# Two-layer hybrid decoder trunk: Silu on ScalarE, two-bank adds into x, and 18 more pairs of the feed-forward blocks computed by seven products

## The chip, the cores and the metric

The kernel runs on one core of one Trainium2 chip. The metric is device time in microseconds (us) of one execution. The kernel before takes 2581.33 us (median of 3 runs, 2581.15 to 2582.71).

A core has engines with instruction queues of their own: TensorE (PE in the profile; PEld is its loading of weights), VectorE (DVE), ScalarE (ACT), GpSimd (POOL) and SyncE (SP, which here issues most of the DMAs). Instructions on one engine run in the order of its queue; engines wait for each other by semaphores. Matmuls write to PSUM, eight banks of 512 fp32 columns by 128 partitions; everything else lies in SBUF.

## The reference, cut to what matters

For `x` of 256 tokens by 2048 columns, in fp32:

- Layer 0: `x += mixer(norm(x))`. The mixer is one input projection (`l0_w_in`, 2048 x 12336), eight mLSTM heads, 32 Mamba-2 (SSD) heads with a short convolution and a gate `y * silu(z)`, and one output projection (`l0_w_out`).
- Layer 1: `x += attention(norm(x))`. With 256 tokens and blocks of 256 this is causal attention over one block, 16 heads of 128 with rotary positions (`l1_w_qkv`, `l1_w_o`).
- After either mixer a feed-forward block: `x += (silu(n @ w_gate) * (n @ w_up)) @ w_down` with `n = norm(x)`, where `w_gate` and `w_up` are 2048 x 5632 and `w_down` is 5632 x 2048.
- A last norm, then the output. Every norm is `x * rsqrt(mean(x*x) + 1e-6) * gain`.

`silu(a)` is `a * sigmoid(a)`, which is also `a/2 * (1 + tanh(a/2))`.

## The kernel before, in words

**Precision.** Every fp32 operand of a large matmul is split in two: a high part, which ScalarE writes by rounding (a copy to the type fp32r), and a low part, which VectorE writes as the operand less the high part. A product is then three matmuls (high by high, high by low, low by high). For a weight tile the high part is `wh` (L439), the low part `wl` (L441); the three matmuls are L472, L473 and L474.

**Tiling.** Activations stand transposed as K tiles (128 of the inner dimension by 256 tokens, high and low), four to a block of a `KT` object. `block` (L456) makes a 256-token by 1024-column result: two strips of 512 columns (of gate and of up in the first half of a feed-forward block, two neighbours elsewhere) by two tiles of 128 tokens, so four PSUM banks F[0] to F[3]. It runs over pairs of K tiles. A pair of kind P costs 4 results x 2 K tiles x 3 matmuls = 24 matmuls of 512 columns. A pair of kind S computes the same 2 x 2 block product with Strassen's (Winograd's form) seven products instead of eight: 7 x 3 = 21 matmuls. For that VectorE makes four sums of the weights (L448, L449, L451: `sums`, which takes a second `raw` buffer), which are split as well, so an S pair has seven weight parts and a P pair four. Four sums of the activations (`skx`, `skh`, by `activation_sums`, L308) are made once for each pair of K tiles. Four of the seven products go into extra banks E (4 to 7); after a block's last S pair they are combined into four tiles `pre` (L510 to L514), which are added to F (L1007) or, with F, into x (L901).

**Plans.** A string tells the kind of each pair of a block. Blocks with 16 K tiles have eight pairs: `PLAN_X` ("PSPSPSPP", three S) for most, `PLAN_LATE` ("PPPSPSPP", two S) for the first block after a norm. `PLAN_H` is for `w_down`: "PSPSPPPP" (two S) for the groups of four hidden strips, "PSPSPP" for the last group of three. While a block is between its first and its last S pair (`held`), the short jobs put off by `later`, such as the transposes of finished hidden strips, are not run, since they use banks 6 and 7.

**A feed-forward block** (`ffn`, L992) goes over 11 hidden strips of 512 columns in groups of 4, 4 and 3. For each strip `hidden` runs one block for gate and up, adds `pre` and F, and makes h with one ScalarE instruction (Tanh, L1010) and two VectorE ones (L1011, L1012). The transposes of h are put off to just after the first pair of the next block. After a group two blocks (`add_blocks`, L893, the two halves of the 2048 columns) multiply by `w_down` and add into x.

**Buffers and order.** Weight tiles come from SyncE's DMAs into `raw` (three buffers and a fourth used every fourth time), `wh` and `wl` (three each). An S pair takes two of each, a P pair one. No order is written out by hand: a scheduler that simulates the program on its own cost model fixes each engine's order beforehand. It follows program order, and `tc.high_priority(offset=n)` lets what is inside go that much earlier (800 for the splits of weights, 1600 for the adds of F). PE's order is rearranged as well: in the trace, parts of a block's first S pair stand behind the next P pair.

**PSUM banks.** The accumulators of the projections that do not use `block` (`lin_w`, `lin_a`) take their banks one by one from a ring of six (`acc_bank`); `block` takes banks 0 to 3 for F. A bank is free for its next user when what is in it has been read.

Of the kernel before, what the change touches and what calls it, by code (L numbers as in the profile page):

```python
# [9 lines left out]
F32 = mybir.dt.float32  # L10
# [30 lines left out]
PLAN_H = {4: "PSPSPPPP", 3: "PSPSPP"}  # L41
# [4 lines left out]
FFN = ({"rawx": 1}, {"skh": 2}, {"blk": 4}, {"gf": 4})  # L46
# [19 lines left out]
def hybrid_trunk(ctx: ExitStack, tc: tile.TileContext, a: dict, out: bass.AP):  # L66
# [88 lines left out]
    ring = {"acc": (0, 1, 2, 3, 4, 5), "aux": (6, 7)}  # L155
# [40 lines left out]
    idle = acc_bank("p_idle")  # L196
# [111 lines left out]
    def activation_sums(a, gains):  # L308
# [6 lines left out]
        nc.vector.tensor_sub(sf[:, 3, :], a12, sf[:, 1, :])  # L315
        if gains:
            sk = small([P, 4, 2, P], "skx", F32R)
        else:
            sk = held_tile("skh", [P, 4, 2, P], "skh", F32R)
        split(sk[:, :, 0, :], sk[:, :, 1, :], sf)  # L320
        return sk

    def sums_of(kt, j):
# [4 lines left out]
        nc.vector.tensor_add(xg, pair[:, :, 0, :].bitcast(F32), pair[:, :, 1, :].bitcast(F32))
        kt.sums[j] = activation_sums(xg, True)
# [40 lines left out]
    def lin_w(w, col, kt, nk, ready=None):  # L370
# [4 lines left out]
        banks = [acc_bank("acc_w") for _ in range(4)]  # L375
# [80 lines left out]
    def block(src, kt, row, nk, plan, after_sums=None, lead=1, pairs=None, ahead=()):  # L456
# [22 lines left out]
        for i_, j in enumerate(order):  # L479
# [58 lines left out]
        return F, pre  # L538
# [354 lines left out]
    def add_blocks(w, kt, row, nk, plans, finish=None, begin=None, whole=None, pairs=None, ahead=((), ())):  # L893

        for q in range(2):
# [3 lines left out]
            def add_all(what):  # L899
                for d, x in zip(dst, what):  # L900
                    nc.vector.tensor_add(d, d, x)  # L901
# [5 lines left out]
            F, _ = block(((w, c0), (w, c0 + STRIP)), kt, row, nk, plans[q], add_all, 2 if final else 1, pairs and list(pairs),  # L907
# [10 lines left out]
            with tc.high_priority(offset=1600):  # L918
                add_all(F)
# [41 lines left out]
    for q in range(2):  # L961
        F, pre = block(tuple((w_in, C_Z + (2 * q + n) * STRIP) for n in range(2)), xt0, 0, KD, PLAN_X if q else PLAN_LATE,
# [29 lines left out]
    def ffn(xt, r, wg_, wu_, wd, name, finish, begin=None, whole=None):  # L992

        rh = cst.tile([P, NT], F32, tag="rh", name="rh" + name)
        rr = cst.tile([P, NT], F32, tag="rr", name="rr" + name)
        nc.vector.tensor_scalar(rh, r, 0.5, None, op0=OP.mult)
        nc.vector.tensor_mul(rr, rh, r)

        def hidden(hT, i, s, plan):
            F, pre = block(((wg_, s * STRIP), (wu_, s * STRIP)), xt, 0, KD, plan)  # L1000
            hs = []
            for t in range(NT):
                g, u = F[2 * t], F[2 * t + 1]
                if pre is not None:
                    for p, f in zip(pre[2 * t:2 * t + 2], (g, u)):
                        with tc.high_priority(offset=1600):
                            nc.vector.tensor_add(p, p, f)  # L1007
                    g, u = pre[2 * t:2 * t + 2]
                h = t2([P, STRIP], "h")
                nc.scalar.activation(h, g, AF.Tanh, scale=rh[:, t:t + 1])  # L1010
                nc.vector.scalar_tensor_tensor(h, h, 1.0, g, op0=OP.add, op1=OP.mult)  # L1011
                nc.vector.scalar_tensor_tensor(h, u, rr[:, t:t + 1], h, op0=OP.mult, op1=OP.mult)  # L1012
                hs.append(h)
# [94 lines left out]
    for q in range(2):  # L1108
        F, pre = block(tuple((w_qkv, 2 * D + (2 * q + n) * STRIP) for n in range(2)), xt2, 0, KD, PLAN_X if q else PLAN_LATE)
# [9 lines left out]
    turn["acc"] = 4  # L1119
# [15 lines left out]
    def begin_ffn1(s):  # L1135
        gain[s] = held_tile("gf", [P, STRIP], "gf")
# [60 lines left out]
```

## Time and profile before

| | |
|---|---|
| median of 3 runs | 2581.33 us |
| profiled execution, span from first to last instruction | 2578.2 us (its time by the measure of the runs isn't given apart; the median lies 3.1 us above its span) |
| PE busy | 2563.5 us, 99% of the span, 12222 matmuls |
| VectorE busy | 2196.5 us, 85% |
| ScalarE busy | 1454.3 us, 56% |
| mean granted TensorE clock | 0.999 |
| DMA | 496.55 MB, mean 193 GB/s |
| first feed-forward block | about 754 to 1460 us of the span |
| second feed-forward block | about 1871 to 2578 us of the span |

How to read it: "busy" is the time in which an engine has at least one instruction under way. Matmuls overlap in the pipeline (one is shown as 0.39 us long while the next starts 0.23 us after it), so a busy PE is no proof that it runs at its best rate; start-to-start times tell that. VectorE's instructions overlap by a little as well. Rows of groups give count, busy time, mean ns of one, then the engine's idle time just before them and what ended it.

### The profile page before, as it was taken

The page shows a single profiled execution, that of the slowest core. Times are in us where ns is not written, and L with a number is a line of the kernel's source. Part 1 is how long each engine was busy: PE and PEld are TensorE (multiplying, and loading weights), DVE is VectorE, ACT ScalarE, POOL GpSimd, SP SyncE. Part 2 cuts the span into 40 slices and gives each one's busy share as a digit, 9 for nine tenths or more (in the row PEclk, how much of TensorE's full clock was granted, in tenths as well). Part 3 has the DMA queues.
Part 4 walks back from the last instruction along what each step waited for, and adds up shares of the span by engine and source line. Part 5 has one row for each costly group of instructions (what it writes and reads, how often), then busy time and mean ns, then how long its engine had stood idle before and what let it go on. Part 6 is the DMA issues. An engine that isn't in the chain of part 4 may idle for free.

```text
span 2578.2 us, 32660 instructions
## 1 busy us (share of the span) xinstructions
PE 2563.5 (99%) x12222; PEld 2130.7 (83%) x12222; DVE 2196.5 (85%) x2831; ACT 1454.3 (56%) x1929; POOL 43.6 (2%) x77
## 2 busy tenths in 40 slices
PE   9999999999999999999999999999999999999998
PEld 8888888888888888888888888888888888888887
DVE  6676777799989998899889986767999888988898
ACT  6465665566665554555455665666655545554554
POOL 2000010000000000000000000000000000000000
PEclk9999999999999999999999999999999999999999
DMA  7566576566564656465656556554555655565554
GB/s 237 170 211 182 166 235 182 163 205 212 185 213 163 215 194 212 163 226 188 206 167 225 186 174 229 164 180 146 180 192 200 212 181 199 193 213 191 199 188 154
DMA packets 254767, 496.55 MB, mean 193 GB/s; under 512 B 15704, under 2 KB 16608, under 8 KB 254352
## 3 DMA queue, kind: packets, MB, share of 16 engines
q1 hardware_dynamic: 250384, 483.26, 57.1%
q0 software_dynamic: 2896, 8.51, 1.1%
q10 hardware_dynamic: 1328, 2.70, 0.3%
q8 instruction: 96, 1.57, 0.2%
q14 instruction: 63, 0.52, 0.1%
HBM read 492.26 MB, written 2.14 MB: 192 GB/s over the span
## 4 chain that ended last, share of the span: by engine, by line
PE 90%; DVE 5%; issue 2%; DMA 2%; ACT 1%; SPq 0%; POOL 0%; POOLq 0%; DVEq 0%; ACTq 0%
PE acc_f L473 18%; PE acc_f L474 18%; PE acc_f L472 17%; PE acc_w L381 11%; PE acc_w L385 5%; PE acc_e L472 4%; PE acc_e L473 4%; PE acc_e L474 4%; PE acc_a L412 2%; PE acc_a L413 2%; PE acc_a L411 2%; DVE wl L441 2%; PE p_tr L282 2%; PE p_y L866 1%; DMA raw<-in_l_w_o 1%
## 5 line engine op out<-in xcount | busy, mean ns | idle before, releaser
L439 ACT CAST wh<-raw 128x1024 fp32r<-128x1024 f32 (+1 forms) x577 | 630.0, 1134 | 412.9 <-PE acc_f L474 338.1
L441 DVE TENSOR_TENSOR wl<-raw,wh 128x1024 fp32r<-128x1024 f32 (+1 forms) x577 | 748.7, 1323 | 79.1 <-ACT wh L439 73.8
L474 PE MATMUL acc_f<-wh,x 128*128 128x512 f32 x1122 | 438.2, 391 | 0.0
L473 PE MATMUL acc_f<-wl,x 128*128 128x512 f32 x1122 | 437.5, 390 | 0.1
L472 PE MATMUL acc_f<-wh,x 128*128 128x512 f32 x1122 | 436.5, 391 | 0.0
L366 DVE TENSOR_TENSOR wl<-raw,wh 128x1024 fp32r<-128x1024 f32 (+1 forms) x225 | 271.3, 1218 | 139.8 <-ACT wh L365 137.3
L439 ACT CAST wh<-sums 128x1024 fp32r<-128x1024 f32 x222 | 227.9, 1051 | 225.9 <-PE acc_f L474 137.7
L365 ACT CAST wh<-raw 128x1024 fp32r<-128x1024 f32 (+1 forms) x225 | 231.9, 1044 | 196.3 <-PE acc_w L381 111.6
L441 DVE TENSOR_TENSOR wl<-sums,wh 128x1024 fp32r<-128x1024 f32 x222 | 266.7, 1221 | 34.6 <-ACT wh L439 34.1
L473 PEld LDWEIGHTS acc_f<-wl,x 128*128 128x128 f32 x1122 | 210.7, 188 | 44.9 <-DVE wl L441 1.9
L474 PEld LDWEIGHTS acc_f<-wh,x 128*128 128x128 f32 x1122 | 210.7, 188 | 43.1
L472 PEld LDWEIGHTS acc_f<-wh,x 128*128 128x128 f32 x1122 | 210.6, 188 | 42.6
L381 PE MATMUL acc_w<-xa,wh 128*128 128x512 f32 x768 | 207.5, 398 | 1.5 <-DVE xa L229 1.5
L381 PEld LDWEIGHTS acc_w<-xa,wh 128*128 128x128 f32 x768 | 138.8, 189 | 27.9 <-DVE xa L229 1.6
L448 DVE TENSOR_TENSOR sums<-raw 128x1024 f32<-128x1024 f32 x111 | 135.4, 1220 | 12.9 <-DMA raw<-in_l_ffn_up 8.0
L381 PE MATMUL acc_w<-x,wh 128*128 128x512 f32 x512 | 138.9, 399 | 0.0
L385 PE MATMUL acc_w<-xa,wl 128*128 128x256 f32 x768 | 121.8, 282 | 0.0
L385 PEld LDWEIGHTS acc_w<-xa,wl 128*128 128x128 f32 x768 | 110.1, 190 | 6.7
L474 PE MATMUL acc_f<-wh,hb 128*128 128x512 f32 (+1 forms) x284 | 109.6, 387 | 0.0
L473 PE MATMUL acc_f<-wl,hb 128*128 128x512 f32 (+1 forms) x284 | 109.6, 387 | 0.0
L472 PE MATMUL acc_f<-wh,hb 128*128 128x512 f32 (+1 forms) x284 | 109.5, 387 | 0.0
L472 PE MATMUL acc_f<-wh,ha 128*128 128x512 f32 x280 | 109.0, 390 | 0.0
(362 smaller groups left out, 4581.3 us busy)
## 6 DMA issues: line engine op xcount, KB each, us to landing
raw<-in_l_w_in SPq DMA_DIRECT2D x191, 512.0 KB, 3.7
raw<-in_l_ffn_gate SPq DMA_DIRECT2D x176, 512.0 KB, 3.9
raw<-in_l_ffn_up SPq DMA_DIRECT2D x176, 512.0 KB, 4.8
raw<-in_l_ffn_down SPq DMA_DIRECT2D x176, 512.0 KB, 5.2
raw<-in_l_w_qkv SPq DMA_DIRECT2D x96, 512.0 KB, 4.7
raw<-in_l_w_out SPq DMA_DIRECT2D x64, 512.0 KB, 5.2
raw<-in_l_w_o SPq DMA_DIRECT2D x32, 512.0 KB, 4.9
rows<-scr POOLq DMA_DIRECT2D x10, 512.0 KB, 5.2
```

The lines of the kernel that those rows point to most:

```text
L282: nc.tensor.transpose(pt[:, j * T + t * P:j * T + (t + 1) * P], src[t][:, c:c + P], ident)
L365: nc.scalar.copy(wh[:, ks, :], raw[:, ks, :])
L366: nc.vector.tensor_sub(wl[:, ks, :], raw[:, ks, :], wh[:, ks, :].bitcast(F32))
L381: return nc.tensor.matmul(banks[f], wh[:, kk, f * P:(f + 1) * P], kt.both(k0 + kk), start=k0 + kk == 0, stop=False, skip_group_check=True)
L385: nc.tensor.matmul(banks[f][:, :T], wl[:, kk, f * P:(f + 1) * P], kt.parts(k0 + kk)[0], start=False, stop=k0 + kk == nk - 1, skip_group_ch ...
L411: nc.tensor.matmul(banks[t], xh[:, ts], wh[:, kk, :], start=k0 + kk == 0, stop=False)
L439: nc.scalar.copy(h[:, c, :], of[:, c, :])
L441: nc.vector.tensor_sub(l[:, c, :], of[:, c, :], h[:, c, :].bitcast(F32))
L448: nc.vector.tensor_sub(sums[:, 0:2, :], raw[:, 2:4, :], raw[:, 3:0:-2, :])
L472: nc.tensor.matmul(dst, ah, bh, start=start, stop=False)
L473: nc.tensor.matmul(dst, ah, bl, start=False, stop=False)
L474: nc.tensor.matmul(dst, al, bh, start=False, stop=stop)
```

## The change

- **Silu.** `Tanh` and the two VectorE instructions after it become `Silu` on ScalarE and one VectorE instruction: in `hidden` L1011 goes away, in the gate of the mixer (L972 to L974) one of two. The two small VectorE instructions at the start of `ffn` that prepared halved scales go too.
- **More S pairs.** `PLAN_H[4]` gets a third S pair (four blocks of a layer, so 8 in all). Hidden strips with an odd number (1, 3, 5, 7, 9 of either layer) run a new `PLAN_X4`, "PSPSSPSP", with a fourth S pair (10 in all): 18 more S pairs and 18 fewer P pairs. The fourth pair of K tiles is number 7; its activation sums are made once a layer, in a buffer of their own (`skx4`). `skh` gets a third buffer.
- **Banks in twos.** Banks 0, 1 and banks 2, 3 become two tiles of two banks each; the ring of accumulators gives banks in twos, and a tile is free when both of its banks have been read. The adds of F into x in `add_blocks` take both banks in one instruction of 1024 columns.
- **Buffers.** The gains of the last norm move from four small buffers into one block buffer (`blk`) that held hidden strips. A pad grows by 16 columns.
- The heading also names low parts by 1024 columns; `weights` isn't touched by the diff, and writes them so already.

```diff
-PLAN_H = {4: "PSPSPPPP", 3: "PSPSPP"}
+PLAN_X4 = "PSPSSPSP"
+PLAN_H = {4: "PSPSPSPP", 3: "PSPSPP"}
...
-FFN = ({"rawx": 1}, {"skh": 2}, {"blk": 4}, {"gf": 4})
+FFN = ({"rawx": 1}, {"skh": 3}, {"skx4": 1}, {"blk": 4})
...
-    def next_bank(kind, name):
-        turn[kind] += 1
-        return bank(ring[kind][(turn[kind] - 1) % len(ring[kind])], name)
-
-    def acc_bank(name):
-        return next_bank("acc", name)
+    def two_banks(i, name):
+        return psm.tile([P, 2, 512], F32, tag=f"q{i}", name=name)
+
+    def acc_banks(name):
+
+        turn["acc"] += 1
+        i = (turn["acc"] - 1) % 3
+        if i == 2:
+            return [bank(4, name), bank(5, name)]
+        both = two_banks(i, name)
+        return [both[:, 0, :], both[:, 1, :]]
...
+        if more:
+            sk = held_tile("skx4", [P, 4, 2, P], "skx", F32R)
+        elif gains:
...
                     if first:
-                        F[i] = bank(i, "acc_f")
+                        if s == 0:
+                            both[t] = two_banks(t, "acc_f")
+                        F[i] = both[t][:, s, :]
...
             with tc.high_priority(offset=1600):
-                add_all(F)
+                add_all(both, wide_dst)
...
-            nc.scalar.activation(th, pre[2 * t + n], AF.Tanh, scale=rh0[:, t:t + 1])
-            nc.vector.scalar_tensor_tensor(th, th, 1.0, pre[2 * t + n], op0=OP.add, op1=OP.mult)
-            nc.vector.scalar_tensor_tensor(piece, th, rh0[:, t:t + 1], piece, op0=OP.mult, op1=OP.mult)
+            nc.scalar.activation(th, pre[2 * t + n], AF.Silu, scale=r0_[:, t:t + 1])
+            nc.vector.tensor_mul(piece, th, piece)
...
-            F, pre = block(((wg_, s * STRIP), (wu_, s * STRIP)), xt, 0, KD, plan)
+            F, pre, _ = block(((wg_, s * STRIP), (wu_, s * STRIP)), xt, 0, KD, plan, pairs=None if plan == PLAN_LATE else (1, 3, 5, 7))
...
-                nc.scalar.activation(h, g, AF.Tanh, scale=rh[:, t:t + 1])
-                nc.vector.scalar_tensor_tensor(h, h, 1.0, g, op0=OP.add, op1=OP.mult)
-                nc.vector.scalar_tensor_tensor(h, u, rr[:, t:t + 1], h, op0=OP.mult, op1=OP.mult)
+                nc.scalar.activation(h, g, AF.Silu, scale=r[:, t:t + 1])
+                nc.vector.scalar_tensor_tensor(h, u, r[:, t:t + 1], h, op0=OP.mult, op1=OP.mult)
...
-                hidden(hT, i, first + i, PLAN_X if first + i else PLAN_LATE)
+                hidden(hT, i, first + i, (PLAN_X4 if (first + i) % 2 else PLAN_X) if first + i else PLAN_LATE)
...
-        gain[s] = held_tile("gf", [P, STRIP], "gf")
+        if s == 0:
+            turn["gains"] = blk([P, 4, STRIP], "gf")
+        gain[s] = turn["gains"][:, s, :]
```

More of the change, by code (lines that the diff above doesn't have):

```diff
@@ L195, in hybrid_trunk @@
     nc.gpsimd.memset(ones, 1.0)
-    idle = acc_bank("p_idle")
+    idle = acc_banks("p_idle")[0]
     turn["acc"] = 0
@@ L306, in turned, with activation_sums @@
                       pv[:, gcol + 4 * b + k:gcol + 4 * b + k + 1])
-    def activation_sums(a, gains):
+    def activation_sums(a, gains, more=False):
         a11, a12, a21, a22 = a[:, 1, :P], a[:, 0, :P], a[:, 1, P:], a[:, 0, P:]
@@ L328, in sums_of @@
         nc.vector.tensor_add(xg, pair[:, :, 0, :].bitcast(F32), pair[:, :, 1, :].bitcast(F32))
-        kt.sums[j] = activation_sums(xg, True)
+        kt.sums[j] = activation_sums(xg, True, len(kt.sums) == 3)
     def transpose_later(kt, b, src, gcol, wait, step=1):
@@ L370, in lin_w @@
     def lin_w(w, col, kt, nk, ready=None):
-        banks = [acc_bank("acc_w") for _ in range(4)]
+        banks = acc_banks("acc_w") + acc_banks("acc_w")
         for k0, wh, wl in chunks(w, col, nk, KC if ready is None else 1):
@@ L403, in lin_a @@
     def lin_a(w, col, kt, nk):
-        banks = [acc_bank("acc_a") for _ in range(NT)]
+        banks = acc_banks("acc_a")
         for k0, wh, wl in chunks(w, col, nk):
@@ L462, in block @@
         n = nk // 2
-        pairs = pairs[:plan.count("S")] if pairs else [j for j in range(n) if plan[j] == "S"]
+        pairs = list(pairs[:plan.count("S")]) if pairs else [j for j in range(n) if plan[j] == "S"]
         rest = [j for j in range(n) if j not in pairs]
@@ L466, in block @@
         F = [None] * 4
+        both = [None] * 2
         pre = None
@@ L537, in block @@
                 held[0] = False
-        return F, pre
+        return F, pre, both
     def sumsq(acc, src, j=None):
@@ L897, in add_blocks, with add_all @@
             dst = [xr_[t][:, c0 + n_ * STRIP:c0 + (n_ + 1) * STRIP] for t in range(NT) for n_ in range(2)]
-            def add_all(what):
-                for d, x in zip(dst, what):
+            wide_dst = [xr_[t][:, c0:c0 + 2 * STRIP].rearrange("p (a b) -> p a b", a=2) for t in range(NT)]
+            def add_all(what, to=dst):
+                for d, x in zip(to, what):
                     nc.vector.tensor_add(d, d, x)
@@ L906, in add_blocks @@
             final = q and whole is not None
-            F, _ = block(((w, c0), (w, c0 + STRIP)), kt, row, nk, plans[q], add_all, 2 if final else 1, pairs and list(pairs),
+            F, _, both = block(((w, c0), (w, c0 + STRIP)), kt, row, nk, plans[q], add_all, 2 if final else 1, pairs and list(pairs),
                          ahead[q])
@@ L961, in hybrid_trunk @@
     for q in range(2):
-        F, pre = block(tuple((w_in, C_Z + (2 * q + n) * STRIP) for n in range(2)), xt0, 0, KD, PLAN_X if q else PLAN_LATE,
+        F, pre, _ = block(tuple((w_in, C_Z + (2 * q + n) * STRIP) for n in range(2)), xt0, 0, KD, PLAN_X if q else PLAN_LATE,
                        ahead=((5, scale_gated, 0),) if q else ((4, sums_of, xt0, 1),))
@@ L992, in ffn @@
     def ffn(xt, r, wg_, wu_, wd, name, finish, begin=None, whole=None):
[L994 to L997, printed above, removed]
         def hidden(hT, i, s, plan):
-            F, pre = block(((wg_, s * STRIP), (wu_, s * STRIP)), xt, 0, KD, plan)
+            F, pre, _ = block(((wg_, s * STRIP), (wu_, s * STRIP)), xt, 0, KD, plan, pairs=None if plan == PLAN_LATE else (1, 3, 5, 7))
             hs = []
             for t in range(NT):
[L1003 to L1008, printed above, removed]
+                g, u = pre[2 * t:2 * t + 2]
+                for p, f in zip((g, u), F[2 * t:2 * t + 2]):
+                    with tc.high_priority(offset=1600):
+                        nc.vector.tensor_add(p, p, f)
                 h = t2([P, STRIP], "h")
-                nc.scalar.activation(h, g, AF.Tanh, scale=rh[:, t:t + 1])
-                nc.vector.scalar_tensor_tensor(h, h, 1.0, g, op0=OP.add, op1=OP.mult)
-                nc.vector.scalar_tensor_tensor(h, u, rr[:, t:t + 1], h, op0=OP.mult, op1=OP.mult)
+                nc.scalar.activation(h, g, AF.Silu, scale=r[:, t:t + 1])
+                nc.vector.scalar_tensor_tensor(h, u, r[:, t:t + 1], h, op0=OP.mult, op1=OP.mult)
                 hs.append(h)
@@ L1108, in hybrid_trunk @@
     for q in range(2):
-        F, pre = block(tuple((w_qkv, 2 * D + (2 * q + n) * STRIP) for n in range(2)), xt2, 0, KD, PLAN_X if q else PLAN_LATE)
+        F, pre, _ = block(tuple((w_qkv, 2 * D + (2 * q + n) * STRIP) for n in range(2)), xt2, 0, KD, PLAN_X if q else PLAN_LATE)
         need("rope")
@@ L1118, in hybrid_trunk @@
     ring["aux"] = (6, 7)
-    turn["acc"] = 4
+    turn["acc"] = 2
     for g in range(4):
```

10 lines of the change are left out of this document (5 added, 5 removed).

## The prediction

> **What bounds the kernel now.** The page first: the busy shares, the clock, the chain that ended last.
>
> ```profile
> span 2578.2 us, 32660 instructions
> ...
> PE 2563.5 (99%) x12222; PEld 2130.7 (83%) x12222; DVE 2196.5 (85%) x2831; ACT 1454.3 (56%) x1929; POOL 43.6 (2%) x77
> ...
> PEclk9999999999999999999999999999999999999999
> ...
> PE 90%; DVE 5%; issue 2%; DMA 2%; ACT 1%; SPq 0%; POOL 0%; POOLq 0%; DVEq 0%; ACTq 0%
> ```
>
> TensorE is busy for 99% at a full clock, and 90% of the chain is its own. Whether a busy TensorE is at its rate, the timeline tells. In hidden strip 1 of the first feed-forward block (FFN) the third S pair begins at 846.13, the next P pair at 850.89, the one after it at 856.33:
>
> ```profile
> 846.13 0.39 PE L472 MATMUL acc_f<-wh,x 128*128 128x512 f32 x1
> 846.36 0.39 PE L473 MATMUL acc_f<-wl,x 128*128 128x512 f32 x1
> ...
> 850.89 0.39 PE L472 MATMUL acc_f<-wh,x 128*128 128x512 f32 x1
> ...
> 856.33 0.39 PE L472 MATMUL acc_f<-wh,x 128*128 128x512 f32 x1
> ```
>
> 21 matmuls in 4.76 us and 24 in 5.44 us: 0.227 us each, without a gap. Next, the view of TensorE's waits. It has seven rows for the whole run, 4.8 us in all, and these two lie near the edited code, one at a seam between stages and one in the first S pair of a hidden strip:
>
> ```profile
> PE p_tr L282 <- DVE pre L514: 0.8, 1, 0.8
> PE acc_e L472 <- DVE hb L226: 0.5, 1, 0.5
> ```
>
> So a matmul taken away is worth its 0.227 us, as long as nobody else gets late. The candidate is VectorE, and its 85% is a mean over unlike stages. By stretches (length, then busy time of PE, PEld, DVE, ACT, POOL; the clock; DMA):
>
> ```profile
> core 0: us, PE busy (x) PEld busy (x) DVE busy (x) ACT busy (x) POOL busy (x), PEclk, DMA share, GB/s
> 859.20:902.00 42.80, 42.80 (x193) 34.76 (x192) 40.84 (x47) 24.14 (x26) 0.00 (x0) 1.00 0.57 196
> 945.30:1072.10 126.80, 126.80 (x563) 104.22 (x562) 109.06 (x116) 62.32 (x63) 0.00 (x0) 1.00 0.61 205
> 754.00:1460.00 706.00, 705.88 (x3156) 577.14 (x3156) 640.61 (x731) 382.31 (x422) 0.70 (x1) 1.00 0.59 196
> ```
>
> The first row is one hidden strip with three S pairs: VectorE is busy for 40.84 of 42.80 us, and only 1.96 us are left. The second row is two `w_down` blocks and one strip: 17.74 us left. The third is the whole first FFN: 91%. That is the kernel's second bound, just under the first, and the S pairs move work from the first to the second.
>
> **The change part by part.** *The 18 S pairs, TensorE's side.* Each saves 5.44 - 4.76 = 0.68 us: 18 x 0.68 = 12.24 us off a path that is TensorE's alone. Eight are in `w_down` blocks, ten in hidden strips.
>
> *Their VectorE side*, from the groups (count, busy us, mean ns):
>
> ```profile
> L441 DVE TENSOR_TENSOR wl<-raw,wh 128x1536 fp32r<-128x1536 f32 x111 | 194.7, 1754 | 4.4 <-ACT wh L439 1.4
> L448 DVE TENSOR_TENSOR sums<-raw 128x1024 f32<-128x1024 f32 x111 | 135.4, 1220 | 12.9 <-DMA raw<-in_l_ffn_up 8.0 <-DMA raw<-in_l_w_o 1.7 <-DMA raw<-in_l_w_out 1.6
> L451 DVE TENSOR_TENSOR sums<-raw,sums 128x512 f32<-128x512 f32 x111 | 76.1, 686 | 0.4
> L449 DVE TENSOR_TENSOR sums<-raw,sums 128x512 f32<-128x512 f32 x111 | 76.1, 685 | 0.3
> L439 ACT CAST wh<-raw 128x1536 fp32r<-128x1536 f32 x111 | 164.8, 1484 | 134.4 <-PE acc_f L474 110.2 <-issue 7.5 <-DMA raw<-in_l_w_o 5.0
> L1011 DVE SCALAR_TENSOR_TENSOR h<-h,pre 128x512 f32<-128x512 f32 x44 | 29.8, 685 | 0.0
> L1010 ACT ACTIVATE h<-pre,rha 128x512 f32<-128x512 f32 x22 | 15.9, 724 | 14.8 <-DVE pre L1007 14.8
> L226 DVE TENSOR_TENSOR skh<-sf,skh 128x512 fp32r<-128x512 f32 x12 | 8.2, 685 | 0.0
> L315 DVE TENSOR_TENSOR sf<-xg,sf 128x128 f32<-128x128 f32 x32 | 9.2, 288 | 0.6
> L901 DVE TENSOR_TENSOR xres<-xres,acc_f 128x512 f32<-128x512 f32 x68 | 45.3, 682 | 11.8 <-PE acc_f L474 11.5
> ```
>
> Both kinds of pair write two low parts of 1024 columns; an S pair adds L448, L449, L451 and the low part of 1536. Instructions in a row overlap, as the timeline shows:
>
> ```profile
> 881.38 2.35 DVE L441 TENSOR_TENSOR wl<-sums,wh 128x1024 fp32r<-128x1024 f32 x2
> 883.65 1.75 DVE L441 TENSOR_TENSOR wl<-raw,wh 128x1536 fp32r<-128x1536 f32 x1
> 885.32 0.69 DVE L451 TENSOR_TENSOR sums<-raw,sums 128x512 f32<-128x512 f32 x1
> ```
>
> Two instructions of 1.22 us take 2.27 us from start to start, so 0.085 us of each is covered. An S pair in place of a P pair costs VectorE 1.22 + 0.69 + 0.69 + 1.75 - 4 x 0.085 = 4.0 us, and ScalarE one cast of 1.48 us out of the 18.66 us that it has free in a strip.
>
> *Silu* takes L1011 away: 2 x (0.685 - 0.085) = 1.2 us of VectorE in each of 22 strips, and as much of the way from the last matmul of a strip to its transposes. Silu itself is not in the trace. Its bounds are L1010's 0.72 us and twice that, as if it took two passes; I take 0.72. Either fits in ScalarE's free time; without that cover it would cost a strip 1.4 us. The gate's eight pieces gain likewise in a stage where I count nothing.
>
> *The ledger.* A strip with four S pairs: VectorE 40.84 + 4.0 - 1.2 = 43.64, TensorE 42.80 - 0.68 = 42.12: **1.52 us too much**. The strip after it, still with three: 39.64 of 42.80, 3.16 us in hand. Together 83.28 of 84.92. For the `w_down` stretch: 109.06 + 2 x 4.0 - 1.2 = 115.9, and one more set of sums of h, 4 x (0.288 - 0.085) + 0.685 - 0.085 = 1.4: 117.3 of 126.80 - 1.36 = 125.4. So the eight pairs in `w_down` are covered, and the ten in the strips only if VectorE carries 1.5 us from a light strip to a heavy one. The whole FFN: 640.61 + 9 x 4.0 - 11 x 1.2 + 2 x 1.4 = 666.2, and 2.0 for the sums of pair 7 (a 512-column add, then as for h), of 706 - 6.1 = 699.9: 95%.
>
> What would be late first is the second half of an S pair's low parts, then TensorE's next products. Whether VectorE can carry is read from what its idle time in such a strip waits for:
>
> ```profile
> 846.37 2.00 ACT L439 CAST wh<-raw 128x1024 fp32r<-128x1024 f32 x2 [1.70 <-PE acc_f L474]
> ...
> 847.46 2.36 DVE L441 TENSOR_TENSOR wl<-raw,wh 128x1024 fp32r<-128x1024 f32 x2 [0.87 <-ACT wh L439]
> ...
> 876.17 1.23 DVE L448 TENSOR_TENSOR sums<-raw 128x1024 f32<-128x1024 f32 x1 [0.74 <-DMA raw<-in_l_ffn_up]
> ```
>
> At 846 VectorE waits for ScalarE, and ScalarE has waited 1.70 us for TensorE to give a `wh` buffer back: all buffers are full, the splits are as far ahead as three buffers allow. Such idle time shrinks when VectorE falls behind. Per heavy strip the loss lies between 0 (all carried) and 43.64 + 1.96 - 42.12 = 3.48 us (nothing carried, all idle time stays). With the buffers full once a strip, and an order that already puts P work ahead of late S products, I take a value near the lower end: 0.3 us, 3.0 us for ten.
>
> *Banks in twos.* An add of 1024 columns (L448: 1.22 us; L901 reads PSUM in 0.682, as fast as the 0.685 of SBUF) replaces two of 0.60: 34 x 0.07 us less for VectorE, nothing on the path. But the last add starts when the fourth result is complete and ends 1.22 - 0.68 = 0.54 us later. Behind it wait, at the three seams where x is normed next, the sums of squares and transposes; 0 to 1.6 us, and I take 0.5, because the first of the waits above (0.8 us) lies at such a seam and P pairs over earlier columns of x cover the rest. In the 20 strips of `lin_w` a bank now waits for its neighbour's reader too:
>
> ```profile
> L419 DVE TENSOR_TENSOR ls<-acc_w,ls 128x256 f32<-128x256 f32 x48 | 19.9, 419 | 0.5 <-ACT ls L418 0.4
> ```
>
> That is 0 to 20 x 0.42 = 8.4 us; none of the seven waits is for such a reader, so there is room, and I take 0.
>
> *Gains, constants, low parts.* The gains' DMAs stand in ScalarE's queue ahead of casts, and wait for a buffer whose last reader is three strips (129 us) back: 0. The low parts by 1024 columns are there already, so 0.
>
> *Table loads.* The trace has one, at the start:
>
> ```profile
> 1.66 1.28 ACT L206 ACT_TABLE_LOAD   x1 [1.66 <-PEq L1186]
> 2.95 0.29 ACT L206 ACTIVATE table<-ident 128x1 f32<-128x1 f32 x1
> ```
>
> If Silu lies in another set than Exp, there are three switches more (gate, softmax, second FFN), 3 x 1.28 = 3.8 us of ScalarE, between 0 and 3.8 on the path; in its free 18.66 us a strip: 0.
> The Trainium skill ("ScalarE: Activation LUTs", What ACT_TABLE_LOAD costs) gives 1283 ns as well, but adds a drain of about 1380 ns, and advises against mixing sets; here the next instruction starts 0.01 us after the load, so this trace shows no drain. By the page's 2.66 us an estimate for three switches would be 8.0 us if all lay on the path, and the sum 2580.6.
>
> **The sum.** Against the span: 2578.2 - 12.24 + 3.0 + 0.5 = 2569.5; the 3.1 us by which the median of the runs stands above it stay: **2572.6 us**.
>
> **The rivals.** *VectorE eats the strips' gain.* Nothing is carried, but its idle time is used: heavy strips run at 43.64, 0.84 over today's, and only `w_down` gains: 2581.3 + 8.4 - 5.4 = 2584.3. For it speak the 1.52 us; against it the full buffers.
> *VectorE becomes the bound with its idle time kept* (the slower side). Heavy strips take 45.60 us, 2.8 more than now: 2581.3 + 28 - 5.4 = 2604. It decides from where a heavy strip takes more than 42.80 + 5.4 / 10 = 43.34 us. Against it: the idle rows come from TensorE's own buffers.
> *Silu's table lacks what stands between* and is reloaded around each: 22 strips x 2 x 2 loads x 1.28 = 113 us of ScalarE; if half delayed the splits, 2572.6 + 56 = 2629. The single load before, for Exp, Tanh, Square and copies together, speaks against it.
> *The three switches lie on the path*: 2572.6 + 3.8 = 2576.4. ScalarE's 18.66 free us a strip speak against it.
> *The edits don't act*: the scheduler turns the freed time of TensorE into waits; by time that is the first rival.
>
> **How the numbers follow.** Forecast (heavy strips lose 0 to 0.8 us each) 0.68; first rival 0.17; the slower one 0.09; reloads 0.03; switches on the path 0.03. About 0.2%, 5.2 us, is what a measurement can tell from no change. The forecast lies below 2576.2 with nearly all of its chance, the first rival and the switches within 5.2 us: faster 0.68, same 0.20, slower 0.12. Lower end: all carried, no seam cost, and the two waits above (1.3 us) gone: 2567.8, rounded to 2567. Upper end: the first rival and a seam's 1.6: 2586. For the forecast alone 2567 to 2577.
>
> **What would show it.** Right: 54 fewer matmuls of 512 columns; heavy strips near 42.1 us and light ones at 42.8; VectorE over 95% busy in both FFNs, with no row of TensorE waiting for `wl` beyond 1 us a strip. Wrong: heavy strips above 43 us, matmuls ended by VectorE's L441; more than four table loads; a wait of over 1 us at a seam.

## The result, and the profile after

The changed kernel takes **2613.7 us** (median of 4 runs, 2612.7 to 2615.0) where the kernel before takes 2581.2: ratio 1.0124, 95% interval 1.0112 to 1.0136. It is 32 us slower; 8.7 us less were forecast. The page of the changed kernel:

```profile
span 2612.3 us, 32564 instructions
...
PE 2569.0 (98%) x12168; PEld 2126.7 (81%) x12168; DVE 2240.1 (86%) x2845; ACT 1490.0 (57%) x1960; POOL 43.8 (2%) x77
...
PEclk9999999999999999999999999999999999999999
...
PE 81%; DVE 9%; DMA 4%; issue 4%; ACT 2%; SPq 0%; POOL 0%; POOLq 0%; DVEq 0%; ACTq 0%
```

The 54 matmuls are gone (12222 to 12168), yet PE is busy for 5.5 us longer, and the chain that ended last is 81% TensorE's instead of 90%, with VectorE at 9% instead of 5%. A "busy" that grows while the work shrinks is one sign that matmuls wait or run slowly inside it. TensorE's idle time, the span less its busy time, goes from 14.7 to 43.3 us. TensorE's waits (us in total, times, the longest), which had seven rows and 4.8 us before; the first eight rows:

```profile
PE acc_e L482 <- ACT wh L448: 5.5, 6, 1.0
PE acc_f L483 <- DVE wl L450: 4.8, 11, 1.3
PE acc_f L482 <- DVE pre L1014: 4.0, 6, 1.6
PE acc_f L482 <- ACT wh L448: 3.6, 1, 3.6
PE acc_e L483 <- DVE wl L450: 3.5, 7, 0.6
PE acc_f L482 <- DVE xres L915: 2.8, 1, 2.8
PE acc_f L482 <- ACT my L235: 1.9, 1, 1.9
PE p_tr L289 <- issue: 1.8, 1, 1.8
```

Now many short waits for split weights (`wh`, `wl`) and for the sums behind a strip, and some long ones at seams. They point at the feed-forward strips, at the banks, and at one single place with 3.6 us. The view by stretches, one row of before and then four of after. The stretch in the first row of each runs from hidden strip 4's activation to strip 8's in the first feed-forward block: four strips, two of them with four S pairs in the changed kernel ("heavy" strips), and two `w_down` blocks.

```profile
core 0: us, PE busy (x) PEld busy (x) DVE busy (x) ACT busy (x) POOL busy (x), PEclk, DMA share, GB/s
1072.10:1327.90 255.80, 255.80 (x1138) 208.93 (x1137) 228.89 (x251) 133.95 (x139) 0.00 (x0) 1.00 0.59 198
```

After:

```profile
1085.40:1344.00 258.60, 255.12 (x1125) 206.80 (x1124) 239.94 (x260) 141.41 (x144) 0.00 (x0) 1.00 0.59 195
1787.80:1934.00 146.20, 140.33 (x638) 115.72 (x637) 127.64 (x185) 87.07 (x138) 0.70 (x1) 0.98 0.50 168
1880.00:1890.00 10.00, 4.34 (x24) 2.90 (x22) 9.84 (x20) 8.89 (x19) 0.00 (x0) 0.87 0.59 209
1890.00:1895.00 5.00, 4.79 (x13) 3.79 (x14) 5.00 (x10) 2.13 (x7) 0.00 (x0) 0.57 0.27 64
```

The first row should have shrunk by 4 x 0.68 us and grew by 2.8; VectorE has 11 us more work there and still 18.7 us idle. The second row of after, from layer 1's `w_o` blocks to its first hidden strip, holds none of the new S pairs. Silu and the wide adds themselves cost what was forecast, and the tables are switched as counted (four loads of 1.28 us each); from the groups:

```profile
L1016 ACT ACTIVATE h<-pre,r 128x512 f32<-128x512 f32 x44 | 31.4, 721 | 51.3 <-DVE pre L1014 51.2
...
L986 ACT ACT_TABLE_LOAD x1 | 1.3, 1283 | 0.0
...
L915 DVE TENSOR_TENSOR xres<-xres,acc_f 128x1024 f32<-128x1024 f32 x34 | 41.1, 1214 | 0.0
```

### The profile page after: what moved, and what is told of

It reads as the page before. It is cut to its first block, busy times and chain, and to the rows that moved or that the text cites. A ratio compares the mean times of both kernels' runs of the same rounds, so it can differ in the third digit from the quotient of the medians.

```text
span 2612.3 us, 32564 instructions
## 1 busy us (share of the span) xinstructions
PE 2569.0 (98%) x12168; PEld 2126.7 (81%) x12168; DVE 2240.1 (86%) x2845; ACT 1490.0 (57%) x1960; POOL 43.8 (2%) x77
## 4 chain that ended last, share of the span: by engine, by line
PE 81%; DVE 9%; DMA 4%; issue 4%; ACT 2%; SPq 0%; POOL 0%; POOLq 0%; DVEq 0%; ACTq 0%
PE acc_f L483 15%; PE acc_f L482 15%; PE acc_f L484 15%; PE acc_w L390 11%; PE acc_w L394 5%; DVE wl L450 5%; PE acc_e L483 3%; PE acc_e L482 3%; PE acc_e L484 3%; DMA raw<-in_l_ffn_up 2%; PE acc_a L420 2%; PE acc_a L421 2%; PE acc_a L422 2%; ACT wh L448 1%; PE p_tr L289 1%
## 5 line engine op out<-in xcount | busy, mean ns | idle before, releaser
L450 DVE TENSOR_TENSOR wl<-raw,wh 128x1024 fp32r<-128x1024 f32 (+1 forms) x559 | 738.2, 1343 | 85.7 <-ACT wh L448 82.3
L482 PE MATMUL acc_f<-wh,x 128*128 128x512 f32 x1062 | 416.5, 393 | 8.8 <-ACT wh L448 3.6
L483 PE MATMUL acc_f<-wl,x 128*128 128x512 f32 x1062 | 416.6, 392 | 1.9 <-DVE wl L450 1.9
L484 PE MATMUL acc_f<-wh,x 128*128 128x512 f32 x1062 | 416.1, 392 | 0.0
L448 ACT CAST wh<-sums 128x1024 fp32r<-128x1024 f32 x258 | 266.1, 1051 | 249.9 <-PE acc_f L484 92.7
L375 DVE TENSOR_TENSOR wl<-raw,wh 128x1024 fp32r<-128x1024 f32 (+1 forms) x225 | 271.0, 1217 | 135.2 <-ACT wh L374 130.6
L450 DVE TENSOR_TENSOR wl<-sums,wh 128x1024 fp32r<-128x1024 f32 x258 | 309.9, 1219 | 22.2 <-ACT wh L448 21.3
L482 PEld LDWEIGHTS acc_f<-wh,x 128*128 128x128 f32 x1062 | 200.7, 189 | 52.6 <-ACT wh L448 7.1
L484 PEld LDWEIGHTS acc_f<-wh,x 128*128 128x128 f32 x1062 | 200.4, 189 | 41.6
L457 DVE TENSOR_TENSOR sums<-raw 128x1024 f32<-128x1024 f32 x129 | 157.3, 1219 | 17.7 <-DMA raw<-in_l_ffn_up 8.4
L483 PE MATMUL acc_e<-wl,skx 128*128 128x512 f32 x291 | 114.2, 392 | 1.4 <-DVE wl L450 1.4
L482 PE MATMUL acc_e<-wh,skx 128*128 128x512 f32 x291 | 112.5, 397 | 1.9 <-ACT wh L448 1.9
L484 PE MATMUL acc_e<-wh,skx 128*128 128x512 f32 x291 | 112.5, 390 | 0.0
L390 PEld LDWEIGHTS acc_w<-x,wh 128*128 128x128 f32 x512 | 92.4, 189 | 16.9
```

What stands on the lines that cost most here:

```text
L375: nc.vector.tensor_sub(wl[:, ks, :], raw[:, ks, :], wh[:, ks, :].bitcast(F32))
L390: return nc.tensor.matmul(banks[f], wh[:, kk, f * P:(f + 1) * P], kt.both(k0 + kk), start=k0 + kk == 0, stop=False, skip_group_check=True)
L448: nc.scalar.copy(h[:, c, :], of[:, c, :])
L450: nc.vector.tensor_sub(l[:, c, :], of[:, c, :], h[:, c, :].bitcast(F32))
L457: nc.vector.tensor_sub(sums[:, 0:2, :], raw[:, 2:4, :], raw[:, 3:0:-2, :])
L482: nc.tensor.matmul(dst, ah, bh, start=start, stop=False)
```

## The experiments

The parts of the change come apart easily, so the first four runs take them one by one; the others look for causes. Differences between runs are taken from their ratios to the kernel before, times 2581 us; the half width of a run's interval is 0.1 to 0.2%, some 2 to 5 us, and a difference of two runs is less certain than either.

### The four parts

**e1**, the changed kernel with single banks:

```diff
-        both = two_banks(i, name)
-        return [both[:, 0, :], both[:, 1, :]]
+        return [bank(2 * i, name), bank(2 * i + 1, name)]
...
-                            both[t] = two_banks(t, "acc_f")
-                            F[i] = both[t][:, s, :]
+                        F[i] = bank(i, "acc_f")
...
-                add_all(both, wide_dst)
+                add_all(F)
```

> The changed kernel with its banks taken one by one again and one add of 512 columns for each bank; Silu and all 18 S pairs stay. Theory A (the S pairs overload VectorE, the banks in twos do nothing): 2610 to 2614 us. Theory B (the banks in twos cost the time outside the hidden strips, some 19 us by the two traces, and the S pairs the rest): 2592 to 2597 us. Theory C (the banks in twos cost all of it, the S pairs pay as forecast): 2569 to 2576 us.

**e2**, the changed kernel without the ten heavy strips:

```diff
-                hidden(hT, i, first + i, (PLAN_X4 if (first + i) % 2 else PLAN_X) if first + i else PLAN_LATE)
+                hidden(hT, i, first + i, PLAN_X if first + i else PLAN_LATE)
```

> The changed kernel with the old plan of three S pairs in every hidden strip (10 S pairs fewer); banks in twos, Silu and the third S pair of the down blocks stay. Theory A: the heavy strips were the cause, 2575 to 2582 us. Theory B: 2596 to 2604 us. Theory C: no gain, 2613 to 2620 us (the ten pairs' 6.8 us lost).

**e3**, e2 with `PLAN_H[4]` back at "PSPSPPPP" as well, so Silu and banks in twos alone:

> The changed kernel without any of the 18 new S pairs: banks in twos and Silu alone. Theory A: 2578 to 2582 us. Theory B: 2594 to 2602 us. Theory C: 2615 to 2626 us.

**e4**, e3 with single banks as in e1, so Silu and the moved buffers alone:

> The kernel before with Silu in place of Tanh and nothing else that acts (no new S pairs, banks one by one). All theories: 2577 to 2582 us. If it is above 2585 us, Silu or the moved buffers cost by themselves (table loads, or another order of the queues).

Measured: e1 2604.4 us, 1.0093 [1.0077, 1.0110]; e2 2576.0, 0.9987 [0.9977, 0.9996]; e3 2583.4, 1.0014 [1.0005, 1.0024]; e4 2573.3, **0.9976 [0.9967, 0.9985]**. In steps from before to after:

```
Silu and buffers        e4 - before   -6.2 us
banks in twos           e3 - e4       +9.8
eight pairs in w_down   e2 - e3       -7.0
ten heavy strips        after - e2   +35.4
```

The heavy strips are the loss, with a smaller one by the banks; Silu, at which nothing was counted, gained (no run parts it from the moved buffers and the third `skh`). e4 came out 4 us below what was expected of it.

**e5**, the changed kernel without its two bad parts (e1's and e2's edits together):

> The changed kernel without its ten four-S strips and without the banks in twos: Silu and the eight new S pairs of the w_down blocks stay. If the parts add up as the first four runs say (Silu alone 2573.3; the eight pairs 2576.0 less 2583.4, that is -7.4), it takes 2564 to 2569, below the kernel before by 0.4 to 0.6%. If the eight pairs gain only beside the paired banks, 2572 to 2576.

**2568.9 us, 0.9952 [0.9937, 0.9967]: faster than both kernels by more than the interval.** The eight pairs gain 6.2 us here too, and the stretch from strip 4 to strip 8, first of e4, then of e5, shows the forecast's 0.68 us apiece (two of them in the stretch: 1.4 us):

```profile
1070.50:1325.40 254.90, 254.90 (x1138) 209.93 (x1137) 223.40 (x244) 133.99 (x138) 0.00 (x0) 1.00 0.58 198
```

```profile
1069.40:1322.90 253.50, 253.50 (x1132) 208.85 (x1131) 232.08 (x256) 138.99 (x142) 0.00 (x0) 1.00 0.60 199
```

e5 is the base for what follows.

### Why the heavy strips cost 35 us

Three causes were open: the order (two S pairs side by side, the last S late), the buffers that S pairs take, and VectorE's load. Each was tried without the others.

**e6** and **e7** move the three S pairs of the ten strips to other places; the work is e5's.

```diff
-PLAN_X4 = "PSPSSPSP"
+PLAN_X4 = "PSPSSPPP"     (e6)
+PLAN_X4 = "PSPSPPSP"     (e7)
```

> e5 with the ten strips' three S pairs at places 1, 3 and 4 (PSPSSPPP) where they were at 1, 3 and 5: as many matmuls, VectorE elements and bytes as e5, but two S pairs stand next to each other, so that four high-part buffers and four raw buffers are wanted of three and four. Theory V (VectorE's sum of work): within 3 us of e5. Theory B (neighbouring S pairs outrun the buffers and the queue behind them): 15 to 38 us above e5.

> e5 with the ten strips' three S pairs at places 1, 3 and 6 (PSPSPPSP): as much work, no neighbours, but the last S pair has one plain pair (5.4 us) behind it, where e5 has two (10.9 us), before the next strip wants the banks that the sums after the last S read. Theories V and B: within 4 us of e5. Theory C (the sums after the last S come too late): 10 us or more above e5.

e6: 2569.0 us, as e5: three S pairs with neighbours cost nothing (their last S comes one place earlier). e7: 2580.9 us, 1.0001 [0.9992, 1.0011], **12.6 us above e5**: a last S pair with one plain pair behind it costs 1.3 us a strip. e11 below finds 9 us for it beside a fourth. What is late there isn't shown: in e7 TensorE's largest sums of waits are for split weights (`wl`, 2.1 and 1.1 us), and none is for the sums behind the last S pair, for which the changed kernel waits 4.0 us (`pre`).

**e8** adds VectorE work and nothing else; **e10** adds the same amount spread out; **e16** and **e17** add a quarter and a half of it. In all four the ten strips keep e5's plan, under a name of its own.

```diff
 h, l = parts(raw, (slice(0, 2), slice(2, 4)))
+for c in (slice(0, 2), slice(2, 4)) * 2:        (e8: the plain pair at place 4)
+    nc.vector.tensor_sub(l[:, c, :], raw[:, c, :], h[:, c, :].bitcast(F32))
...
+nc.vector.tensor_sub(l[:, 2:4, :], raw[:, 2:4, :], h[:, 2:4, :].bitcast(F32))
+   (e10: places 2, 4, 6 and 7; e17: 4 and 7; e16: 4)
```

> e5 with the low part of the plain pair at place 4 of the ten strips written three times over: 4 more subtractions of 1024 columns, about 4.2 us of VectorE in one place, where the fourth S pair put 4.0, with no S pair, matmul or buffer changed. Theory V: the ten strips need 3.2 us of idle VectorE and more, so they stretch and e8 is 10 to 40 us above e5. Theory B: within 5 us of e5.

> e5 with the same 4.2 us of VectorE more in each of the ten strips as e8, in four single operations: the plain pairs at places 2, 4, 6 and 7 each write the second half of their low part twice. If VectorE's sum over the strip decides, within 6 us of e8 (2594.2): 2588 to 2600. If it is that a low part came 4 us late at one place, 2569 to 2578.

> e5 with one more subtraction of 1024 columns (1.05 us of VectorE) in each of the ten strips, a quarter of e10's load: the second half of the low part at place 4 is written twice. e10 cost 29.3 us. If any load on VectorE costs in proportion, a quarter of it: 2575 to 2578. If VectorE's 3.2 us of idle time in a strip takes it up, 2568 to 2571.

> The same with two (places 4 and 7, 2.1 us a strip, half of e10's load), which is still less than the 3.2 us of idle VectorE of a strip of e5. In proportion: 2582 to 2586. If the idle time takes it up whole, 2568 to 2572; if the idle time can only be used in part, between them.

```
VectorE added per strip   0 (e5)   1.05 (e16)   2.1 (e17)   4.2 (e10)   4.2 (e8, one place)
time, us                  2568.9   2569.7       2571.1      2598.1      2594.2
ratio to before           0.9952   0.9957       0.9964      1.0071      1.0049
```

The first line is what was planned; by VectorE's busy time in the stretch from strip 4 to strip 8, which holds two such strips, it was 1.1, 2.15, 4.4 and 4.4 us each. The cost does not grow in proportion: the first 2.1 us a strip cost 3 us in all (the intervals of e17 and e5 overlap), the next 2.1 cost 28. (e10 also adds at places 2 and 6, which e17 leaves alone, so amount and place are not parted between these two; e8, with the full amount at place 4 alone, speaks for the amount.) Each of these strips had 3.2 us of idle VectorE. The stretch from strip 4 to strip 8 says the same; e17 and e10:

```profile
1070.50:1324.20 253.70, 253.70 (x1132) 208.65 (x1131) 236.38 (x260) 139.02 (x143) 0.00 (x0) 1.00 0.59 199
```

```profile
1074.60:1333.60 259.00, 257.13 (x1131) 207.01 (x1131) 240.90 (x264) 138.33 (x143) 0.00 (x0) 1.00 0.59 195
```

VectorE busy for 236.4 us costs 0.2 us against e5, 240.9 costs 5.5, although 18 us of it stay idle. In e10 the loss stands behind the loaded strips more than in them. Hidden strip 1 and the stretch of two `w_down` blocks and strip 4 in e10, then the latter in e5:

```profile
815.60:858.40 42.80, 42.80 (x193) 34.98 (x192) 40.29 (x47) 24.09 (x27) 0.00 (x0) 1.00 0.50 170
...
944.80:1074.60 129.80, 127.78 (x559) 102.98 (x558) 117.19 (x124) 65.90 (x65) 0.00 (x0) 1.00 0.61 203
```

```profile
943.90:1069.40 125.50, 125.50 (x558) 103.70 (x558) 113.57 (x121) 65.70 (x64) 0.00 (x0) 1.00 0.61 201
```

By the starts of the activations the ten strips with the added work take 0.1 to 0.8 us longer than in e5, the four stretches behind them 3.7 to 4.5 us each, though VectorE has 12.6 us idle in the one shown. So VectorE's lateness is carried on, and is paid a little later instead of being made up. In e8, where the work comes in one place, the loss is in the strips themselves, as TensorE's waits tell; L456 is the subtraction written over again, L232 the split of h:

```profile
PE acc_f L485 <- DVE wl L456: 11.4, 10, 1.5
PE acc_e L484 <- DVE hb L232: 2.5, 2, 1.4
PE acc_e L484 <- DVE ha L232: 1.9, 2, 1.3
```

These 15.8 us are most of e8's 25; there the late low part itself is one wait for each strip.

**e11** and **e12** go the other way, from the heavy strips: e11 is e1 with the four S pairs early, e12 is e11 with VectorE relieved. In e12 the low parts of two plain pairs of each heavy strip are left out, and their matmuls read the high part again.

```diff
-PLAN_X4 = "PSPSSPSP"
+PLAN_X4 = "PSSPSSPP"
...
+            if bare:                 (e12: plain pairs at places 3 and 6 of heavy strips)
+                for c in cuts:
+                    nc.scalar.copy(h[:, c, :], of[:, c, :])
+                return h, h
```

> e1 (Silu, w_down pairs, single banks, four-S strips: 2604.4) with the four S pairs of the ten strips at places 1, 2, 4 and 5 (PSSPSSPP): as much work, the last S one place earlier, with two plain pairs behind it. If VectorE's load and the late last S add up (e8 cost 25.4, e7 12.0, the saved products 6.8), it gives the 12 back: 2590 to 2595. If neighbouring S pairs are dear once there are four, 2604 to 2620.

> e11 without the low parts of the plain pairs at places 3 and 6 of the ten strips: their products read the high part twice, so that TensorE and ScalarE do as much as in e11 and VectorE 4.2 us less per strip, about what it does in e5. The part of the computation left out is these low parts. If VectorE's load is the cause: e5 less ten times 0.68, 2560 to 2566. If the S pairs themselves, their buffers or their transfers are: within 6 us of e11.

e11: 2595.6 us, 1.0058 [1.0043, 1.0073], 9 us below e1: the late last S again. e12: 2572.7 us, 0.9969 [0.9958, 0.9981], **23 us below e11**. The edit takes away VectorE's work and, with it, two low-part buffers a strip and the waits for them; e8 and e10, which add work and no buffers, say that the work alone is enough. Strip 4 to strip 8 of e11, then of e12:

```profile
1077.70:1333.10 255.40, 253.69 (x1126) 207.43 (x1125) 239.67 (x264) 141.88 (x144) 0.00 (x0) 1.00 0.59 198
```

```profile
1070.70:1323.00 252.30, 252.30 (x1126) 207.64 (x1125) 230.68 (x256) 141.89 (x144) 0.00 (x0) 1.00 0.60 200
...
1155.40:1197.40 42.00, 42.00 (x190) 34.45 (x189) 38.88 (x46) 25.89 (x28) 0.00 (x0) 1.00 0.62 203
1762.60:1904.00 141.40, 137.56 (x627) 113.57 (x626) 125.47 (x187) 86.03 (x137) 1.67 (x1) 0.99 0.49 165
```

With VectorE at e5's load the stretch is 1.2 us shorter than e5's and a heavy strip takes 42.00 us against 42.60: 0.60 of the 0.68 us saved are there to be had. Not all of the 23 us is waiting for VectorE itself. In e11 the granted clock falls at three places:

```profile
920.00:930.00 10.00, 7.33 (x21) 5.48 (x22) 5.87 (x10) 3.79 (x5) 0.00 (x0) 0.66 0.50 173
1870.00:1880.00 10.00, 7.47 (x21) 5.72 (x22) 9.71 (x18) 8.57 (x20) 0.00 (x0) 0.66 0.30 105
2020.00:2030.00 10.00, 8.40 (x26) 6.34 (x27) 5.87 (x11) 4.73 (x6) 0.00 (x0) 0.66 0.39 131
```

By these rows that is at most 3.4 us each, an estimate; e12 has one such place, half as long, and e8 and e10 have none before their tails. e12 was expected at 2560 to 2566. Its last row shows one place of the missing time: from `w_o` to the first hidden strip of layer 1, TensorE is idle for 3.8 us. The same stretch of e5:

```profile
1762.80:1899.30 136.50, 135.98 (x630) 112.59 (x629) 125.25 (x187) 87.07 (x137) 0.70 (x1) 1.00 0.53 176
```

e5 has no such gap, and no heavy strip runs there in either.

### A place in the ring

Every kernel with heavy strips lost 5 to 9 us in that stretch. What differs when it begins is, as far as the plans tell, only which of the `raw`, `wh` and `wl` buffers comes next: the five additional S pairs of layer 0 take five more of each. **e13** and **e14** put the counters where e5 has them (for `wl`, 2 in e14, where plain pairs skipped some):

```diff
     ffn(xt1, r1, a["l0_ffn_gate"], a["l0_ffn_up"], a["l0_ffn_down"], "a", finish)
+    turn["wh"] += 1
+    turn["wl"] += 1
+    for _ in range(3):
+        turn["spare"] += 1
+        if turn["spare"] % 4 != 3:
+            turn["raw"] += 1
```

> The changed kernel (2613.7) with the counters that pick the next raw, high and low buffer moved on by 3, 1 and 1 places between the two feed-forward stages, so that layer 1 starts them where the kernel without four-S strips does (five more S pairs in layer 0 leave them elsewhere). Theory R (the place of the ring costs the stretch from the o strips to the first hidden strip of layer 1 its 5 to 9 us, which every four-S kernel but no other shows): that stretch falls from 146.1 to 137 to 141 and the time to 2604 to 2610. Otherwise 2612 to 2616.

> e12 (low parts of the plain pairs at places 3 and 6 of the ten strips left out, 2572.7) with the same move of the buffers' counters. Theory R: the stretch from the o strips to the first hidden strip falls from 141.6 to 136 to 137 and the time to 2566 to 2569, which leaves only the first two four-S strips of each layer above e5. Otherwise 2571 to 2574.

e13, the changed kernel so: **2598.8 us, 1.0070 [1.0055, 1.0085], 13.9 us less** by no other edit. e14: 2566.2 us, 0.9945 [0.9930, 0.9960], 6.2 less than e12. The stretch in e13, then in e14:

```profile
1781.40:1918.60 137.20, 137.20 (x637) 114.04 (x636) 126.64 (x185) 87.23 (x137) 0.70 (x1) 1.00 0.54 179
```

```profile
1766.10:1901.90 135.80, 135.80 (x630) 112.50 (x629) 125.09 (x187) 87.04 (x137) 0.70 (x1) 1.00 0.51 173
```

146.2 us became 137.2 (e2, without heavy strips, has 137.2 as well), and 141.4 became 135.8, TensorE without a gap and at full clock in both. So the place in the ring is worth 9.0 and 5.6 us here. The rest of e13's gain is not all the counters'. Its last `w_down` blocks of layer 0, up to the first qkv matmul, are 3.6 us shorter than in the changed kernel; the order of the instructions begins to differ within them. Up to there the two traces show the same instructions in the same order, yet from hidden strip 0's activation to strip 10's e13 takes 602.9 us and the changed kernel 607.7; only the latter has a drop of the clock on the way, at 870 us. e14 lies the other way: over the same strips, with the same instructions, it takes 2.6 us more than e12. So a few microseconds between two runs of a kernel with heavy strips need no cause in the edit. Which of the three rings decides wasn't tried.

e14 is also only 1.8 us below e5, where the ten strips' products should give 6.8. Hidden strips 1 to 3 of layer 0 in e14, then in e5:

```profile
816.30:948.30 132.00, 129.22 (x569) 104.69 (x568) 119.52 (x142) 76.50 (x81) 0.00 (x0) 0.99 0.58 192
```

```profile
815.80:943.90 128.10, 128.09 (x574) 105.05 (x574) 118.21 (x136) 73.25 (x79) 0.00 (x0) 1.00 0.58 198
```

e12, with the same instructions there, takes 129.4 us. So something beside VectorE's load and the ring still costs in the first heavy strips, and not the same in every run; it was not isolated.

### The banks in twos

**e9** is e2 with one add for each bank; the tiles stay two banks long.

```diff
-                add_all(both, wide_dst)
+                add_all(F)
```

> e2 (Silu, the w_down pairs, banks in twos, no four-S strips: 2576.0) with one add of 512 columns for each bank again, where e2 has one of 1024 for two; the tiles stay two banks long. If the wide adds are what the banks in twos cost, 2567 to 2571 as e5; if it is that a tile of two banks is handed on as one, within 2 us of e2.

2573.4 us, 0.9970 [0.9959, 0.9982], half way between e2 (0.9987) and e5 (0.9952): the wide adds cost about 4.4 us and the tiles handed on as one about 4.6. Neighbouring intervals overlap, so the sum of 9.0 is firm and the split is not. TensorE's waits of e2, which e5 hasn't:

```profile
PE acc_f L482 <- DVE xres L915: 4.0, 2, 2.8
PE acc_f L482 <- ACT my L235: 1.9, 1, 1.9
PE p_tr L289 <- issue: 1.8, 1, 1.8
```

By the starts of the first matmuls, e2 is behind e5 by 3.8 us before the first `lin_a` strip, by 3.3 more when the mixer's projection reaches `my`, by 1.9 at the first hidden strip and by 1.9 in the next two seams (1.5 come back at the end); inside the feed-forward strips and `w_down` blocks, where most of the 34 wide adds are, it gains nothing (253.3 against 253.5 us from strip 4 to strip 8).

### Can another engine take the load?

**e15** is e11 with the low parts that e12 left out computed by GpSimd.

```diff
+            low = nc.gpsimd if by_pool else nc.vector
...
-                nc.vector.tensor_sub(l[:, c, :], of[:, c, :], h[:, c, :].bitcast(F32))
+                low.tensor_sub(l[:, c, :], of[:, c, :], h[:, c, :].bitcast(F32))
```

> e11 (four early S pairs, 2595.6) with the low parts of the plain pairs at places 3 and 6 of the ten strips computed by GpSimd instead of VectorE, nothing left out. No run here shows GpSimd at such an operation. If it takes less than about 5 us for 1024 columns and leaves VectorE alone, as e12: 2566 to 2575. If it is slower or holds VectorE up, above 2595.

2638.4 us, 1.0225 [1.0208, 1.0242]. Its groups, its waits, and VectorE's own subtractions (shortest, median, longest in ns):

```profile
L450 POOL TENSOR_TENSOR wl<-raw,wh 128x1024 fp32r<-128x1024 f32 x40 | 115.6, 2910 | 1074.4 <-ACT wh L448 1054.9 <-DVE wl L450 19.4
```

```profile
PE acc_f L483 <- POOL wl L450: 37.6, 30, 1.9
```

```profile
L450 DVE TENSOR_TENSOR wl<-sums,wh x258: 1212/1221/3374, 531.9 to 2611.5; 128x1024 fp32r<-128x1024 f32 x129
```

GpSimd needs 2.91 us for what takes VectorE 1.22, TensorE waits for it, and VectorE's own instruction of the same size lasts up to 3.37 us, where the longest in e11 is 1.23. The Trainium skill ("SBUF — State Buffer", two separate sides) describes an exclusive lock on a port pair that the two engines share, held for a whole instruction. The stretched instructions agree with it, though no run here shows the lock by itself.

## Why the prediction was wrong

**TensorE's price: right.** 0.68 us for each pair, 54 matmuls fewer. e5's `w_down` blocks gave 0.70 us a pair and e12's strips 0.60 where nobody was late.

**The ledger: right in kind.** A heavy strip wants more VectorE than TensorE (43.64 against 42.12); `w_down` is covered. e8, e10 and e17 place the edge where a ledger puts it, between 2.1 and 4.2 us more for 3.2 us idle.

**The carrying, "a value near the lower end: 0.3 us": the step that failed.** In e13, where the ring costs nothing, the ten strips still cost 21.5 us against e2, and they saved 6.8, so each lost 2.8 us by load and lateness, of a possible 0 to 3.48 that the text had. By the starts of the activations, 14.7 us of it lie in the heavy strips and 9.4 in the four stretches of two `w_down` blocks and a strip behind them. The reading behind the choice was that VectorE's idle time before a cast that waits for TensorE shrinks when VectorE falls behind. In e10 VectorE kept 18 us idle over four strips and two `w_down` blocks while TensorE lost 5.5: the lateness went on into the next stretch, and the idle time there did not make it up before TensorE had to wait. How the lateness passes through the four engines and their buffers in detail was not isolated. The rival with VectorE as the bound and its idle time kept (2604, chance 0.09) had this mechanism, and its sum was nearest. That is in part luck: its heavy strips of 45.60 us were not reached (44.0 on average in e13), and it holds neither the ring nor the banks.

**Left out: the plan's last S pair.** "PSPSSPSP" also moves the last S pair one place later. e7 prices that alone at 12.6 us for ten strips, e11 against e1 at 9. The text costed how many instructions an S pair has, not where its sums come due. Two costs that meet in one strip do not simply add: 30.7 and 12.6 less 6.8 would be 36.5, against 21.5 measured in e13. (With single banks, e1 less e5, it is 36.4, but with the ring's 5.0 us in it and with three drops of the clock.)

**Left out: the ring.** 9.0 us, in the stretch behind the `w_o` blocks, by which buffer comes next; e13 as a whole is 13.9 us faster. "More S pairs" was costed in the strips in which they are; what they shift behind them was not looked at.

**Banks in twos, 0.5 us: too small by a factor of 16 to 20.** 8.0 us (after less e1) to 9.8 (e3 less e4), some half by the tiles (for the neighbour's reader the text had 0 to 8.4 us and took 0; no row of waits names it) and half by the wide adds at seams (0 to 1.6, took 0.5). That no row of waits before named such a reader showed that it wasn't late then; it did not show how much later it could come.

**Silu: price right, gain missed.** 721 ns as Tanh, four table loads, none on the path. But the 1.2 us less of VectorE in each strip were put into the ledger only. Together with the moved buffers, from which no run parts them, they took 6.2 us off the time: from activation to activation a strip took 42.8 to 43.6 us with Tanh and 42.6 to 42.9 in e4, and the first one of layer 1 went from 42.9 to 41.3.

**Of what was to show it**, "heavy strips above 43 us" and "a wait of over 1 us at a seam" came true (nine of the ten, 43.2 to 46.5 us from activation to activation; 2.8 and 3.6 us), and matmuls did wait for `wl`, 18 times and 8.3 us in all. "VectorE over 95%" did not: it was 93% in the stretch shown, and that was already too much.

## What to carry to other kernels

An engine that is second by a few per cent had room here for some 2 us of the 3.2 idle in a strip; idle time in the stretches behind, or 7% of a whole stage, was no reserve. So price a load strip by strip and take the bad end where a strip's sum is over. Before costing a new plan at so many instructions each, ask what its order makes late and where its rings of buffers stand when it is done; moving three counters gave back 9.0 us in one stretch. Parts of a change belong on the chip one by one: two of these four made a kernel that is 0.48% faster, all four one that is 1.2% slower.

## What the runs showed of the hardware that was not expected

**A long wait costs twice: the granted clock drops behind it.** The timeline of the changed kernel at the 3.6 us wait, TensorE's instructions:

```profile
1887.68 1.22 PE L482 MATMUL acc_f<-wh,x 128*128 128x512 f32 x2 [3.62 <-ACT wh L448]
1890.21 0.79 PE L483 MATMUL acc_f<-wl,x 128*128 128x512 f32 x1 [1.31 <-DVE wl L450]
1890.80 0.63 PE L484 MATMUL acc_f<-wh,x 128*128 128x512 f32 x1
1891.23 0.63 PE L482 MATMUL acc_f<-wh,x 128*128 128x512 f32 x1
```

After it the matmuls start 0.43 us apart where 0.227 is usual, and the granted clock in the row of 1890 to 1895 above is 0.57. The page's line of the clock, in 40 slices, shows only nines: a few microseconds at half rate do not lower a slice of 65 us below nine tenths. The kernel before, whose waits come to 4.8 us in all, shows no such drop between its first microseconds and its tail. The Trainium skill ("TensorE: Matmul & The Clock Gate", Part 1: The HAM clock gate) has a half rate after an idle window of about 3.4 us and 426.7 ns for 512 columns at it; the 0.43 us and the wait of 3.62 us agree. But the same trace has the half rate after shorter waits as well:

```profile
868.52 0.50 PE L482 MATMUL acc_e<-wh,skx 128*128 128x512 f32 x1 [0.96 <-ACT wh L448]
870.65 0.79 PE L482 MATMUL acc_f<-wh,x 128*128 128x512 f32 x1 [1.62 <-DVE pre L1014]
871.24 0.63 PE L483 MATMUL acc_f<-wl,x 128*128 128x512 f32 x1
871.67 0.63 PE L484 MATMUL acc_f<-wh,x 128*128 128x512 f32 x1
```

Here two waits of 0.96 and 1.62 us with one matmul between them come before it, and at 1502 us one of 2.81 us does. So no unbroken wait of 3.4 us is needed, and several short waits close together can cost more than their sum.

**Where a ring stands is worth 5.6 and 9.0 us** in one stretch of kernels that are the same otherwise (e14, e13).

**GpSimd's subtraction** of 128 x 1024 columns takes 2.91 us against VectorE's 1.22, and lengthens some of VectorE's (e15).
